# Two token parts from the input projection on, and 224 gathered tokens, in a hybrid decoder step with attention, recurrence and 16384 experts

## The chip, the cores and the metric

The kernel runs on one core of a Trainium2 chip. The metric is the device time of one execution in microseconds (us). The core's engines are TensorE (PE in the profile, its weight loads PEld), VectorE (DVE), ScalarE (ACT), GpSimd (POOL) and SyncE (SP), whose queue issues most DMAs.

## The reference, cut to what matters

One decoder layer is applied to 512 prompt tokens and 32 sample tokens (8 sequences of 4), 544 in all, with a model width of 2048.

```python
h = rmsnorm(x)                          # all 544 tokens
q, k, v, iq, ik, iw, xb, yb, qm = split(h @ w_in)
# A) each query scores all earlier keys (16 small heads), keeps the best 128 and attends to them;
#    sample tokens see 512 cached keys as well
# B) width-4 causal convolution of xb, two gates, linear recurrence over time, times gelu(yb)
# C) attention of qm to 256 memory tokens, 4 heads
m = sum(sigmoid(h @ w_gate[n]) * (branch[n] @ w_br[n]) for n in range(3))
x = x + m @ w_o
z = rmsnorm(x); q = z @ w_peer_q        # 8 heads x 2 halves x 128
# per head and half: top 16 of 128 keys; top 16 of the 256 sums -> 16 experts of 16384 per head
act = gelu(peer_u[e] . z);  x = x + sum(softmax(score) * act * peer_v[e])
y = rmsnorm(x)
```

The outputs are y, and keys, values, indexer keys, convolution and recurrence states and the memory's keys and values.

## The kernel before

All matrices are kept with tokens as columns. A float32 product is made of three TensorE products: `split` (L218) makes a high half on ScalarE (`hi`, L219) and a low half on VectorE (`lo`, L220), and high x high, high x low and low x high are summed in PSUM. `stream` (L236) loads 128 x 1024 weights (512 KB) through SP's queue and splits them. `project` (L254) takes two such loads for 2048 inputs; each of its 16 blocks gives three matmuls per group of token columns. 544 tokens are two halves of 272 columns, `xF` and `xA` (L303 to L306).

The order of work is that of the program text. Work in generators is woven in by `Background` (L138): `pump` is called once for each of the 8 blocks of a weight load and adds an eighth of `rate` steps; three queues (`bg`, `bg2`, `bg3`) have rates of their own, and `drain` runs what is left of one. `urgent` (L222) puts instructions ahead of others that are ready.

The stages, in order:

- Memory keys and values, with the first norm behind them.
- Input projection: 45 blocks of 128 outputs (`in_proj`, L400), both halves of tokens for each weight. Memory attention (`mem_head`, `mem_sample`), the scores and choice of keys (`dots`, `select_prompt`, `select_sample`), attention (`attn_head`, `attn_sample`) and the recurrence (`lru`) are background work of all tokens. It is drained at L644 and at L819.
- First half: `merge` (L833) of the three branches with their gates, `output_proj` (L875), then the query projection and the expert choice, `Route` (L950), of 256 of the 272 tokens; the other 16 queries are kept (`qk`). `lists` finds the top 16 of 128 keys per head half and tile of 128 tokens, `head` combines two lists. `pairs` (L1064) projects the queries and lets at most three `head` generators wait.
- Second half: merge and output projection. In its first branch (`after_merge`, L1183) the first choice is drained and the gather begins.
- Gather (`gathered`, L1115): the first 192 tokens don't go through all experts. Their rows of u and v are fetched by indirect DMAs issued by GpSimd (L1094), 128 rows of 8 KB each, and VectorE multiplies and sums them (L1142, L1150). 128 tokens take 128 slots; 64 tokens lie twice on the partitions and take 64. It is background `bg3`: a step fetches one slot's rows and works on one fetched two steps ago. `pace` ties a step to the last matmul.
- Second choice: the other 288 tokens in three tiles, the queries interleaved with `up` (L1215), the product of an expert block of 128 with the remaining 352 tokens. 50 of 128 ups are stored to DRAM ahead.
- Gate matrices (`gate_matrix`, L1227): for each token a one-hot product (L1259) spreads 128 weights over 128 x 128 experts, four tokens to a PSUM bank, which ScalarE copies into `gs` with another order (L1260).
- Dense experts: 16 rounds of 8 ups, the gating (`gated`, L1326) and the down products (`down`, L1344, matmul L1353) of 352 columns; last the norm and the output.

## Time and profile before

| | us |
|---|---|
| median of 3 runs | 4478.11 |
| lowest and highest | 4473.07, 4478.17 |
| profiled execution, its time | 4504.29 |
| profiled execution, its span | 4502.5 |

The span is from the first to the last instruction of one execution. The profile gives the busy time of each engine, the chain of work that ended last (followed back from the last instruction), groups of instructions by line with the mean duration of one, and the busy times in chosen stretches together with the granted clock of TensorE and the busy share of the 16 DMA engines. Matmuls follow each other before the one ahead has left the array, so the pace of a matmul is taken from the length of a chain piece over its count, not from the duration of one.

### The profile page before, as it was taken

To read this page: it belongs to the slowest core of one execution; us is meant where nothing else is said; L and a number is where in the kernel's file an instruction comes from. 1 tells how busy PE (TensorE), PEld (TensorE's weight loads), DVE (VectorE), ACT (ScalarE), POOL (GpSimd) and SP (SyncE) were. 2 spreads that over 40 slices of the span, in tenths; PEclk is the share of its full clock that TensorE was granted. 3 is DMA by queue.
4 is the path that set the end of the run, shared out by engine and by line. 5 is a ranking of instruction groups with operands and counts; after the bars stand their busy time and mean duration, and the time that the engine had idled before them with its cause. 6 is when DMAs were issued, how large, how long until landed. Compare 5 with 4: busy or idle time off the path is not lost.

```text
span 4502.5 us, 74141 instructions
## 1 busy us (share of the span) xinstructions
PE 4299.6 (95%) x29249; PEld 4130.8 (92%) x29249; DVE 3214.8 (71%) x4876; ACT 1823.1 (40%) x2732; POOL 1228.6 (27%) x1072
## 2 busy tenths in 40 slices
PE   8999989999999989998899899899999999999998
PEld 7986878789999989998888899899999999999998
DVE  6334825344456887887788776788888887888886
ACT  6232226544344434444332896222333333333333
POOL 3001110410001333533243101233343332344333
PEclk9999999999999999999999999999999999999999
DMA  8423443355556559998755676999999988999994
GB/s 267 164 85 116 145 131 107 120 161 185 178 183 209 166 165 336 360 351 302 273 169 168 208 253 238 352 343 330 335 337 349 349 309 302 349 345 345 347 352 154
DMA packets 342447, 1118.56 MB, mean 248 GB/s; under 512 B 42641, under 2 KB 137745, under 8 KB 289361
## 3 DMA queue, kind: packets, MB, share of 16 engines
q1 hardware_dynamic: 282704, 700.65, 45.8%
q0 software_dynamic: 59392, 413.17, 24.9%
q8 instruction: 229, 3.75, 0.3%
q14 instruction: 122, 0.99, 0.1%
HBM read 1050.75 MB, written 62.87 MB: 247 GB/s over the span
## 4 chain that ended last, share of the span: by engine, by line
PE 81%; DVE 7%; DMA 4%; issue 3%; ACT 2%; POOL 2%; another core or an unknown queue 1%; SPq 0%; DVEq 0%; POOLq 0%; ACTq 0%
PE mm L269 54%; PE mm L1353 19%; DVE lo L220 2%; PE w L1259 1%; PE mm L370 1%; PE w L556 1%; DMA gl<-ge_dram 1%; DMA x2r<-x_dram 1%; POOL eq L1017 1%; PE w L499 1%; POOL cand L1003 1%; ACT hi L219 1%; DVE eq L1015 1%; PE w L797 0%
## 5 line engine op out<-in xcount | busy, mean ns | idle before, releaser
L219 ACT CAST hi<-raw 128x1024 fp32r<-128x1024 f32 x1050 | 1096.8, 1049 | 1722.5 <-PE mm L269 898.8
L220 DVE TENSOR_TENSOR lo<-raw,hi 128x1024 fp32r<-128x1024 f32 x1050 | 1310.8, 1251 | 593.5 <-ACT hi L219 565.2
L269 PE MATMUL mm<-xgd,hi 128*128 128x352 f32 (+1 forms) x4608 | 1109.3, 324 | 10.5 <-ACT hi L219 10.5
L269 PEld LDWEIGHTS mm<-xgd,hi 128*128 128x128 f32 x4608 | 799.5, 189 | 14.3 <-ACT hi L219 12.4
L269 PE MATMUL mm<-xgd,lo 128*128 128x352 f32 (+1 forms) x2304 | 744.3, 323 | 32.9 <-DVE lo L220 32.9
L269 PE MATMUL mm<-xF,hi 128*128 128x272 f32 x2976 | 701.5, 295 | 2.8 <-issue 2.1
L1353 PE MATMUL mm<-zh,hi 128*128 128x352 f32 x2048 | 664.0, 326 | 29.3 <-ACT zh L219 20.9
L269 PE MATMUL mm<-xA,hi 128*128 128x272 f32 x2976 | 688.4, 290 | 1.7 <-ACT hi L219 1.3
L1353 PE MATMUL mm<-zh,lo 128*128 128x352 f32 x2048 | 664.0, 325 | 3.7 <-DVE lo L220 3.7
L1353 PE MATMUL mm<-zl,hi 128*128 128x352 f32 x2048 | 665.2, 325 | 1.8 <-DVE zl L220 1.8
L1094 POOL DMA_INDIRECT row<-in_un,idx x192 | 377.8, 1968 | 851.4 <-PE mm L269 333.7
L1094 POOL DMA_INDIRECT row<-in_vn,idx x192 | 391.0, 2036 | 680.8 <-PE mm L269 238.3
L269 PEld LDWEIGHTS mm<-xF,hi 128*128 128x128 f32 x2976 | 514.4, 189 | 39.2 <-issue 36.4
L269 PEld LDWEIGHTS mm<-xA,hi 128*128 128x128 f32 x2976 | 516.0, 190 | 10.5 <-issue 7.5
L1142 DVE SCALAR_TENSOR_TENSOR row<-row,xnat 128x2048 f32<-128x2048 f32 x192 | 440.2, 2293 | 64.2 <-DMA row<-in_un,idx 19.6
L1150 DVE SCALAR_TENSOR_TENSOR gacc<-row,hv,gacc 128x2048 f32<-128x2048 f32 x190 | 446.5, 2350 | 37.1 <-PE mm L269 13.9
L269 PEld LDWEIGHTS mm<-xgd,lo 128*128 128x128 f32 x2304 | 434.4, 189 | 38.2 <-DVE lo L220 37.9
L269 PE MATMUL mm<-xA,lo 128*128 128x272 f32 x1488 | 434.2, 292 | 10.0 <-DVE lo L220 9.9
L269 PE MATMUL mm<-xF,lo 128*128 128x272 f32 x1488 | 432.3, 291 | 0.0
L1353 PEld LDWEIGHTS mm<-zh,hi 128*128 128x128 f32 x2048 | 387.4, 190 | 33.5 <-ACT zh L219 23.3
L1353 PEld LDWEIGHTS mm<-zh,lo 128*128 128x128 f32 x2048 | 387.9, 190 | 5.5 <-DVE lo L220 5.5
L1353 PEld LDWEIGHTS mm<-zl,hi 128*128 128x128 f32 x2048 | 387.9, 189 | 3.2 <-DVE zl L220 2.9
(365 smaller groups left out, 6215.6 us busy)
## 6 DMA issues: line engine op xcount, KB each, us to landing
raw<-in_u SPq DMA_DIRECT2D x256, 512.0 KB
raw<-in_v SPq DMA_DIRECT2D x256, 512.0 KB
raw<-in_w_gate SPq DMA_DIRECT2D x192, 512.0 KB
raw<-in_w_br SPq DMA_DIRECT2D x96, 512.0 KB
raw<-in_w_in SPq DMA_DIRECT2D x90, 512.0 KB
raw<-in_w_pq SPq DMA_DIRECT2D x64, 512.0 KB
raw<-in_w_o SPq DMA_DIRECT2D x64, 512.0 KB
g_dram<-gs SPq DMA_DIRECT2D x11, 2048.0 KB
```

The lines of the kernel that those rows point to most:

```text
L219: nc.scalar.copy(hi, src)
L220: eng.tensor_tensor(lo, src, hi.bitcast(F), op=OP.subtract)
L269: last["mm"] = nc.tensor.matmul(p[:, i, :n], a[:, s], chunk(b[which], u + k), start=(u + k == 0 and pr == 0), stop=(u + k == k_chunks - 1 ...
L370: nc.tensor.matmul(p[:, mt], a[:, k, m], w[:, i * 512:(i + 1) * 512], start=(k == 0 and pr == 0), stop=(k == ND - 1 and pr == 2))
L499: nc.tensor.matmul(p[32 * c:32 * c + 32, j * 256:(j + 1) * 256], eT[:, i, 32 * h:32 * h + 32], cv[:, i, h * 256:(h + 1) * 256], start=(i = ...
L556: nc.tensor.matmul(p[:, :nk], s[r, P0 + qb * 128:P0 + qb * 128 + 128], ik2[r, P0:P0 + nk], start=True, stop=True)
L1003: nc.gpsimd.tensor_tensor(c2[:, :, :, off:off + n], lists[1][:, :, :, :n], lists[0][:, :, :, i:i + 1].to_broadcast([128, 2, nt, n]), op=OP ...
L1015: nc.vector.tensor_tensor(eq, iota[:, None, :ncand].to_broadcast([128, 16, ncand]), F16[:, t, :, None].to_broadcast([128, 16, ncand]), op= ...
L1094: i = nc.gpsimd.indirect_dma_start(out=r, out_offset=None, in_=ins[table], in_offset=bass.IndirectOffsetOnAxis(ap=ind[:, s:s + 1], axis=0))
L1142: j = nc.vector.scalar_tensor_tensor(r, r, 1.0, xn, op0=OP.mult, op1=OP.mult, accum_out=h)
L1150: j = nc.vector.scalar_tensor_tensor(acc, r, h, acc, op0=OP.mult, op1=OP.add)
L1353: last["mm"] = nc.tensor.matmul(p[:, 0, :NTA], a[:, s], b, start=(k == 0 and pr == 0), stop=(k == 7 and pr == 2))
```

## The change

Tokens are cut into 288 (32 sample and 256 prompt tokens, `HA`) and 256 (`HB`) instead of 272 and 272. The whole input projection with its attention, memory and recurrence work becomes a function `branches(part)`, called for part 0, then merge, output and expert choice of the first part run, and then `branches(1)`. What the second part needs of the first (keys, values, indexer keys, the last convolution inputs, the recurrence state) is kept in SBUF. Each weight of the input projection is streamed once for each part. The first choice has three tiles (128, 128, 32 tokens) and the second two, and `qk` goes. The gather starts in `branches(1)`, at the fourth memory head. 224 tokens are gathered in units of 128, 64 and 32, the last with four copies of the tokens on the partitions; 320 go through the dense experts. In the gate matrices the four tokens of a bank are written interleaved. Rates of the background queues and some extra buffers change.

```diff
-HT = T // 2
+HA = NS + SEQ // 2
+HB = T - HA
-NG = 192
+UNITS = ((0, 128, 1), (128, 64, 2), (192, 32, 4))
+NG = 224
...
+    kps = ExitStack()
+    kp_ = pool("keep", kps, side="right")
+    kT = kp_.tile([128, 2, T], F, name="kT")
...
+    def branches(part):
+        first = part == 0
+        x, cols, p0, qbs = ((xF, slice(0, HA), P0, (0, 1)), (xA, slice(HA, T), 0, (2, 3)))[part]
+        pp = None if first else ps_p
...
         def in_proj(ch, dst):
-        p = project(ins["w_in"][ch], [xF, xA], ND)
+            p = project(ins["w_in"][ch], [x], ND, pp)
...
+        left = bg.queue[-1] if bg.queue else None
+        bg.rate = 1.1 if first else 2.0
+        for h in range(4):
+            if h == 3 and not first:
+                bg.drain(left)
+                route1.weights()
+                start_gather()
+                rps.close()
+                bg3.rate = 0.5
+                bg.rate = 1.0
...
-    bg2.rate = 3.3
+        bg2.rate = 1.8
...
+        bg.rate = 2.5
+        bg2.rate = 2.2 if first else 1.6
...
-    tiles1 = [(0, 128), (128, 128)]
-    tiles2 = [(0, 128), (128, 128), (256, 32)]
+    tiles1 = [(0, 128), (128, 128), (256, 32)]
+    tiles2 = [(0, 128), (128, 128)]
...
-    widen(wide, 1, 1)
-    pairs(route1, query1, lambda c: None)
+    widen(wide, 1, 0)
+    pairs(route1, lambda c: query(c, xgF), lambda c: None)
...
+    branches(1)
...
-    mA = merge(HT, xA, map_, "left", after_merge)
+    mA = merge(HA, xA, map_, "left")
...
             for j in range(4):
-                nc.tensor.matmul(p[:, j * 128:(j + 1) * 128], o2[:, j], o1[:, j], start=True, stop=True)
-            nc.scalar.copy(gs[:, :, q * 4:q * 4 + 4].rearrange("p i t -> p t i"),
-                           p.rearrange("p (t i) -> p t i", t=4))
+                nc.tensor.matmul(p.rearrange("p (i t) -> p i t", t=4)[:, :, j], o2[:, j], o1[:, j], start=True, stop=True)
+            nc.scalar.copy(gs[:, :, q * 4:q * 4 + 4], p.rearrange("p (i t) -> p i t", t=4))
...
-    bg.rate = 1.3
-    bg3.rate = 0.15
+    bg.rate = 1.2
+    bg3.rate = 0.3
...
-    bg3.rate = 0.3
+    bg3.rate = 0.7
     for j in ups:
         up(j)
...
     for g in range(16):
-        bg3.rate = 0.7 if 8 * g < AHEAD_UP else 0.74
+        bg3.rate = 0.68 if 8 * g < AHEAD_UP else 0.7
```

## Rows read from the trace of the kernel before

**Rows 1.** The page, its head and the engines' busy us, share, instructions.
```profile
span 4502.5 us, 74141 instructions
PE 4299.6 (95%) x29249; PEld 4130.8 (92%) x29249; DVE 3214.8 (71%) x4876; ACT 1823.1 (40%) x2732; POOL 1228.6 (27%) x1072
```
**Rows 2.** Chain that ended last: start us, us, what, count (256, 512, 272, 352, 352 columns).
```profile
38.36 31.55 PE mm L269 x263
72.23 42.34 PE mm L370 x186
955.29 526.61 PE mm L269 x4207
...
3742.66 16.94 DMA xnat<-xn_dram
4245.10 62.72 PE mm L269 x384
4307.82 61.47 PE mm L1353 x384
```
**Rows 3.** Stretches: engines' busy us (instructions), TensorE's granted clock, DMA share, GB/s.
```profile
114.00:955.00 841.00, 806.81 (x5424) 674.69 (x5423) 378.85 (x852) 309.94 (x502) 124.63 (x151) 0.98 0.39 124
1482.00:1612.00 130.00, 118.26 (x912) 115.98 (x911) 113.08 (x404) 51.25 (x100) 51.48 (x121) 0.97 0.48 147
1612.00:2060.00 448.00, 433.27 (x3415) 430.44 (x3414) 368.33 (x433) 193.91 (x250) 195.77 (x132) 1.00 0.87 318
2190.00:2500.00 310.00, 273.83 (x1794) 262.98 (x1795) 252.42 (x771) 96.45 (x147) 106.74 (x196) 0.97 0.50 164
2500.00:2758.00 258.00, 253.86 (x1773) 252.04 (x1772) 197.10 (x369) 251.21 (x527) 23.02 (x14) 0.99 0.69 243
2828.00:3200.00 372.00, 346.98 (x2070) 340.11 (x2071) 316.64 (x365) 111.17 (x138) 125.15 (x61) 0.97 0.95 342
3200.00:3650.00 450.00, 450.00 (x2783) 450.00 (x2782) 393.18 (x390) 148.28 (x179) 169.30 (x85) 1.00 0.94 346
```
**Rows 4.** Groups by line, VectorE, 3250 to 3650 us: busy us, mean ns, idle before.
```profile
L220 DVE TENSOR_TENSOR lo<-raw,hi 128x1024 fp32r<-128x1024 f32 x103 | 125.6, 1220 | 11.2 <-ACT hi L219 11.1
L1150 DVE SCALAR_TENSOR_TENSOR gacc<-row,hv,gacc 128x2048 f32<-128x2048 f32 x40 | 94.0, 2351 | 5.7 <-PE mm L1353 2.1 <-PE mm L269 2.0 <-DMA row<-in_vn,idx 1.4
L1142 DVE SCALAR_TENSOR_TENSOR row<-row,xnat 128x2048 f32<-128x2048 f32 x36 | 82.4, 2288 | 15.6 <-DMA row<-in_un,idx 7.6 <-PE mm L1353 5.6 <-PE mm L269 2.3
L1356 DVE TENSOR_TENSOR acc<-mm,acc 128x352 f32<-128x352 f32 x48 | 25.0, 520 | 10.1 <-PE mm L1353 10.1
```
**Rows 5.** Groups by line, VectorE, 1480 to 1660 us.
```profile
L1015 DVE TENSOR_TENSOR eq<-cst,f 128x800 f32<-128x800 f32 x16 | 20.2, 1280 | 0.1
L960 DVE FIND_INDEX8 j<-si,sc 128x8 uint32<-128x128 f32 x32 | 9.0, 282 | 0.0
L1019 DVE TENSOR_REDUCE ev<-eq 128x16 f32<-128x800 f32 x8 | 7.8, 971 | 3.3 <-POOL eq L1017 3.3
L960 DVE FIND_INDEX8 p<-t,cand 128x8 uint32<-128x50 f32 x16 | 3.2, 203 | 0.0
L960 DVE MATCH_VALUE_LOAD j<-si,sc 128x8 f32 x32 | 2.4, 74 | 0.0
```
**Rows 6.** Groups by line, ScalarE, TensorE and VectorE, 2500 to 2758 us.
```profile
L1260 ACT COPY gs<-w 128x512 f32<-128x512 f32 x87 | 94.7, 1096 | 0.9 <-PE w L1259 0.9
L219 ACT CAST hi<-raw 128x1024 fp32r<-128x1024 f32 x44 | 46.6, 1058 | 0.5 <-PE mm L269 0.5
L269 PE MATMUL mm<-xgd,hi 128*128 128x352 f32 x707 | 179.6, 336 | 0.0
L1259 PE MATMUL w<-o,o 128*128 128x128 f32 x700 | 94.3, 277 | 4.1 <-DVE o L1276 4.0
L1269 DVE TENSOR_TENSOR o<-cst,Ti 128x512 f32<-128x512 f32 x88 | 60.2, 684 | 3.0 <-PE w L1259 2.9
```
**Rows 7.** The stretch from 1950 to 2000 us, columns as in rows 3.
```profile
1950.00:2000.00 50.00, 50.00 (x400) 50.00 (x399) 46.15 (x48) 23.87 (x32) 22.00 (x15) 1.00 0.98 378
```

More of the change, by code (lines that the diff above doesn't have):

```diff
@@ L278, in inv_rms @@
             for i in range(2):
-                nc.tensor.matmul(acc[:, i, :HT], ones, ssum[:, i * HT:(i + 1) * HT], start=True, stop=True)
-            a, o = acc[:, :, :HT], halves(out)
+                nc.tensor.matmul(acc[:, i, :n // 2], ones, halves(ssum)[:, i], start=True, stop=True)
+            a, o = acc[:, :, :n // 2], halves(out)
         else:
@@ L392, in program @@
-    nc.sync.dma_start(c1, ins["cst"][:, CB:])
-    def k1(a, n, rows=slice(0, 128)):
-        return c1[rows, a - CB:a - CB + n]
-    def bt(a):
-        return a[:, :P0].rearrange("p (b t) -> p b t", b=NB)
-    def in_proj(ch, dst):
-        p = project(ins["w_in"][ch], [xF, xA], ND)
-        with urgent():
-            nc.scalar.copy(halves(dst), p)
-        nc.sync.dma_start(outs["proj"][ch], dst)
-    def staged(ch):
-        s = stg.tile([128, T], F, name="stage", bufs=5)
-        in_proj(ch, s)
-        return s
@@ L490, in mem_sample @@
             for i in range(2):
-                nc.tensor.transpose(p[:, i * 128:(i + 1) * 128], e[:, i * 128:(i + 1) * 128], ident)
-            eT = mp.tile([128, 2, SEQ], F, name="mpT")[:, :, :128]
-            nc.scalar.copy(eT, p[:, :MEM].rearrange("p (a b) -> p a b", a=2))
+                for k in range(5):
+                    r = slice(0, 128 if k < 4 else NS)
+                    nc.tensor.matmul(p[:64, i * 256:(i + 1) * 256], pT[r, k, 64 * i:64 * i + 64],
+                                     vp[i][:, k] if k < 4 else vS, start=(k == 0), stop=(k == 4))
@@ L494, in mem_sample @@
+            oN = bp.tile([64, 512], F, name="oN")
+            nc.scalar.copy(oN, p[:64])
             yield
-            p = ps_w.tile([128, 512], F, name="w1")
-            for h in range(4):
-                c, j = divmod(h, 2)
+            for n in range(2):
+                r = slice(32 * n, 32 * n + 32)
+                p = ps_w.tile([128, 512], F, name="w1")
                 for i in range(2):
-                    nc.tensor.matmul(p[32 * c:32 * c + 32, j * 256:(j + 1) * 256], eT[:, i, 32 * h:32 * h + 32],
-                                     cv[:, i, h * 256:(h + 1) * 256], start=(i == 0), stop=(i == 1))
-                if h == 1:
-                    yield
@@ L515, in mem_sample @@
-        nc.sync.dma_start(o_dram[16:24, :, :P0].rearrange("h p s -> p h s"), mT)
-    bg.rate = 1.0
-    for h in range(4):
-        qm = []
-        for i in range(2):
-            s = staged(CH_QM + 2 * h + i)
-            nc.vector.tensor_copy(qms[:, 2 * h + i], s[:, :P0])
-            qm.append(s)
-        bg.add(mem_head(h, qm))
-    bg.add(mem_sample())
-    ik = xp_.tile([128, T], F, name="ik")
-    in_proj(CH_IK, ik)
-    ik2 = xp_.tile([128, T], F, name="ik2")
-    nc.scalar.copy(ik2[0:64], ik[0:64])
@@ new lines, in branches @@
+        if first:
+            bg2.add(*[attn_sample(pr) for pr in range(NB // 2)])
+        bg.rate = 2.5
+        bg2.rate = 2.2 if first else 1.6
+        for c in range(8):
+            xb = staged(CH_XB + c)
+            yb = staged(CH_YB + c)
+            bg.add(lru(c, xb, yb))
+        bg2.drain()
+        bg.drain()
+        if first:
+            nc.sync.dma_start(o_dram[0:8, :, :P0].rearrange("h p s -> p h s"), osm)
+        else:
+            nc.sync.dma_start(outs["hout"].rearrange("c p n -> p c n"), hl)
@@ L831, in program, with merge @@
+        lrs.close()
+        br.close()
     GLAG = 2
-    def merge(c0, x, mp_, side, each=None):
+    def merge(c0, x, mp_, side):
         mo = ([], [])
+        n_ = x[0].shape[-1]
         os_ = ExitStack()
         op_ = pool(f"lm{c0}", os_, side=side)
-        m = [mp_.tile([128, HT], F, name=f"m{e}", tag="ml", bufs=ND + 1) for e in range(ND)]
+        m = [mp_.tile([128, n_], F, name=f"m{e}", tag="ml", bufs=ND + 1) for e in range(ND)]
         for i, n in enumerate((2, 0, 1)):
-            op = ([op_.tile([128, HT], R, name=f"oh{k}") for k in range(8)],
-                  [op_.tile([128, HT], R, name=f"ol{k}") for k in range(8)])
+            op = ([op_.tile([128, n_], R, name=f"oh{k}") for k in range(8)],
+                  [op_.tile([128, n_], R, name=f"ol{k}") for k in range(8)])
@@ L902, in program @@
     xgfp = pool("xgf", xgfs, side="right")
-    xgF = [xgfp.tile([128, ND, HT], R, name=f"xgF{i}") for i in range(2)]
-    output_proj(0, mF, xgF, 0, rs[:, :HT])
+    xgF = [xgfp.tile([128, ND, HA], R, name=f"xgF{i}") for i in range(2)]
+    output_proj(0, mF, xgF, 0, rs[:, :HA])
     mfs.close()
@@ L1123, in gathered @@
             xn = gp.tile([128, D], F, name="xnat")
[L1124 to L1125 removed]
+            for a in range(0, 128, n):
+                nc.sync.dma_start(xn[a:a + n], xn_dram[c0 - 128:c0 - 128 + n])
         nb = slots // blk
```

906 lines of the change are left out of this document (471 added, 435 removed).

## The prediction

> **What bounds the kernel now.** I read the page first. Its profiled execution spans 4502.5 us, of which TensorE is busy 95% [rows 1]; that run took 4504.3 us as a whole, and the median of the runs shown is 4478.1, so 26 us below it. My sum is made against 4502.5 us and its difference is then put on the median.
>
> Next comes the chain of work that ended last, for the pace of TensorE where nothing interrupts it [rows 2]. Dividing each piece by its count gives one matmul of 256 columns 120.0 ns, of 272 columns 125.2, of 352 columns 163.3 in the up products and 160.1 in the down products, of 512 columns 227.6. From 272 to 512 that is 0.427 ns a column, close to one column per cycle at 2.4 GHz (0.417), with about 12 ns on top. Weight loads are as many as matmuls and stay beneath them.
>
> Then the busy times by stage [rows 3]: input projection with the attention behind it (114 to 955 us), second merge (1612 to 2060), the expert choice of the two halves (1482 to 1612 and 2190 to 2500), gate matrices (2500 to 2758), the first part of the down products, reading stored ups (2828 to 3200), and the loop of ups and downs (3200 on). The reader is to see two things. In the long stages TensorE is full. But VectorE stands at 87% in both the first expert choice and the loop, and DMA at 0.94 to 0.95 of its share with 342 to 346 GB/s. So TensorE is the bound with two followers close behind, and the change takes work from TensorE and gives work to both.
>
> **The change, part by part.** (1) *Dense experts.* The gathered tokens go from 192 to 224, so the dense matmuls go from 352 to 320 columns. 128 ups and 128 downs of 48 matmuls each are 12288 matmuls; 32 columns at 0.417 ns are 13.3 ns, in all 164 us off the path. By the step from 272 to 352 columns [rows 2] a column is 0.476 ns (up) or 0.436 (down), so up to 179 us. I take 164: ups 149.9 ns, downs 146.7.
>
> The Trainium skill, "TensorE: Matmul & The Clock Gate", section on the back-to-back issue gap, speaks against this: in a stream of weight load and matmul pairs it gives about 81 ns at 128 columns and 131 at 512, so 0.13 ns a column, and 32 columns would save only about 51 us, by which my sum below would end at 4533 (an estimate from that page). The 120, 125, 163 and 228 ns of this trace disagree.
>
> (2) *The extra gathers.* Slots go from 128 + 64 to 128 + 64 + 32, each with a row of u and one of v: 64 more rows of 128 x 8 KB. On VectorE a row costs 2.32 us, the mean of the two kinds [rows 4], so 148 us; GpSimd pays about 2 us each for issuing, and has time (169 of 450 us [rows 3]). Each is 1.05 MB, in all 67 MB.
>
> (3) *The input projection in two parts.* 45 chunks x 48 x 2 matmuls stay 4320, now 288 and 256 columns. 288 columns cost 125.2 + 16 x 0.417 = 131.9 ns, so a pair costs 251.9 ns where it cost 250.4: 3 us here; the merge, output and query matmuls were split before and go from 272/272 to 288/256, in all 7 us more. Of that the first part gets 4224 x 6.7 = 28 us more ahead, the second 22 us less. The weights are streamed twice: 90 more loads on SP's queue (47 MB), 90 more halvings on ScalarE and 90 x 1.22 = 110 us on VectorE. Small operations (recurrence, attention) come twice at half width.
>
> (4) *Order.* The gathers can start behind the first expert choice, which now lies ahead of the second part's projection, so about 39 of the 472 steps of the gather run there (78 weight streams x 0.5), 88 in the second merge and output, and the rate in the loop falls from 0.70/0.74 to 0.68/0.70. Counting streams times rates to the end gives 476 steps for 472, so nothing much is left over behind the last product.
>
> (5) *First choice with three tiles, second with two.* A tile costs VectorE per query chunk two searches, two maxima and a replacement with three loads, 5 x 0.28 + 3 x 0.07 = 1.6 us; per head the same five over a list of 50 at 0.2 each with loads, 1.24, then 1.28 and 0.97, together 3.5 us [rows 5].
>
> (6) *One-hot products.* TensorE writes PSUM with a stride of four, ScalarE reads it straight and writes runs of four. The copy takes 1.10 us [rows 6] where the plain copy to the high half, of twice the size, takes 1.06 [rows 6], so it should come down to about 0.6, for 80 copies instead of 88: up to 45 us of ScalarE, which is busy 251 of 258 us there [rows 3]. No strided TensorE write is in the trace; I bound it by 0 and by a doubling of 640 matmul records at 0.115 us (74 us), a gain being excluded as the columns stay as many, and take 0, since a write stays one element per column. (The 0.115: TensorE's 253.9 us [rows 3] less 707 and half as many again of 352 columns at 163.3 ns, over 700 records [rows 6].) The copy's bounds are 0.5 and 1.1 us. One group of 32 tokens less spares 64 records, 7 us.
>
> **The sum by stage** (before to after, profiled us).
> - Input projection, 841. Before, 4320 x 125.2 = 541 us are streams and 300 attention on TensorE and its stalls. I split these by keys and sample tokens (an estimate): 87 of matmuls to the second part, 195 with stalls to the first, which becomes 285 + 195 = 480. Second part: TensorE 259 + 87 = 346. VectorE there: 110 for halvings; half of the 379 [rows 3] less as many halvings, about 140; three left-over heads at 11, 33; 39 rows, 92: 375, less some 6% by which successive instructions overlap (an estimate), 352. The engines come out level and the two places where a chain is drained stay, and I take 397. The start of the gather adds a wait: VectorE's copy of the reshuffled indices waits for small DMAs, and the low halves queue behind it; 0 to the 16.9 us of a reload that held the chain [rows 2], which I take as nothing, three weights being ready. Together 877: **+36** (bounds 0 to +80).
> - First merge and output: **+28**.
> - First choice, 130 us with VectorE at 113 [rows 3]. It gets 16 x 1.6 + 5 heads x 3.5 = 43 us more (three heads may stay behind), and nothing covers that: TensorE's own 101 us are shorter already. **+43** (20 to 65).
> - Second merge, 448: TensorE 3456 x 5.2 ns = 18 less, heads no longer in its way 13 less, DMA fuller 10 more: **-21**. Output: **-8** (768 x 5.2 ns = 4, and waits).
> - Second choice, 310 with VectorE at 252: a tile less (-50), twice the gathers (+25), so 227 against TensorE's 257 (768 x 120 ns, 22 ups at 7.2, some 8 of lists). TensorE loses 4 on queries and 21 ups x 48 x 13.3 = 13, and about 18 of its 36 us of idle: **-35** (-10 to -45).
> - Gate matrices, 258: VectorE 197 - 11 (8 of 88 one-hot pairs at 0.68 [rows 6] and as much again) + 15 more rows x 2.32 = 217 after the shorter halvings, TensorE 147 + 74 = 221. So VectorE takes ScalarE's place. At 92% it needs 236; later ups move in. **-12** (-30 to +10).
> - Dense part, 2828 to the end. TensorE gives 78 ups x 48 x 13.3 + 128 x 48 x 13.3 = 132. Taken back: for each of the first 50 expert blocks DMA needs 2 streams of 0.524 MB, 1.43 MB of gathers, 0.33 of gates and stored ups, 2.80 MB in 7.04 us, 398 GB/s, where 342 was reached with stalls [rows 3]. At 350 the 50 take 400 us instead of 352; before it lost some 32, so 16 more are lost. In the loop VectorE per block was 15.5 x 0.874 = 13.6 us, and loses 0.16 gathers x 2.32 and 0.17 for five tiles narrowed from 352 columns at 0.52 us [rows 4]: 13.0 in 14.2, 92%. DMA: 2.10 + 2.94 + 0.16 = 5.20 MB in 14.2 us, 366 GB/s. I take 14 us of stalls, and 10 for one more change of gather unit (its reload held the chain 16.9 us [rows 2]). **-92** (-132 to -20).
>
> All: 36 + 28 + 43 - 21 - 8 - 35 - 12 - 92 = -61, so 4478 - 61 = 4417, rounded to **4420 us**. What TensorE saves is thus mostly paid back on VectorE.
>
> **The rivals.** *A, all is covered.* VectorE and DMA run at 92% to 98% without holding TensorE. For it: from 1950 to 2000 us VectorE was at 92%, DMA at 0.98 and 378 GB/s, and TensorE never stopped [rows 7]. Against it: the first choice has no cover at all. Then only the matmuls count: -164 + 10 - 7, 4317, and with the first choice 4360.
>
> *B, VectorE becomes the bound everywhere: slower.* It can't hold more than the 87.4% of the loop, the highest share that TensorE stood over hundreds of us. Its place is every stage with gathers, and it decides as soon as VectorE's work exceeds 0.874 of TensorE's, which is so in five of them. First choice 175/0.874 = 200 (+27 on my sum), second part's projection +30, second choice +10, gates +13, the two dense parts 355/0.874 and 1019/0.874, +6 and +32: 118 more, 4538. Against it: [rows 7].
>
> *C, DMA saturates at the loop's 346 GB/s* [rows 3]. Second merge and output at 364 GB/s asked, 507 us: +26 against 10 counted; first 50 blocks 140 MB/346 = 405, +5; loop 406 MB/346 = 1172, against 1108 + 14: +50. Together about +71, 4490: about no change. Against it 378 GB/s in [rows 7]. The Trainium skill, "DMA: Bandwidth & Descriptors", section "Where 436 GB/s comes from", takes the HBM side, about 358 GB/s per core, to bind such transfers; by that the loop's stage would take 1134, near my own (an estimate from that page). The 378 of [rows 7] goes above it.
>
> *D, matmuls shorten less than their columns do*, weight loads setting part of the pace. The smallest step of the rows, from 256 to 272 columns, is 5.2 ns for 16 columns, 0.325 each; 12288 x 32 of these are 128, 36 less than counted: 4456. A pace set by the loads alone would save nothing and give 4584; the four durations of [rows 2], which grow all the way, exclude that. The page named under (1) lies between.
>
> **How the numbers follow.** My forecast 0.60 (alone 4370 to 4475), A 0.13, B 0.15, C 0.11, D 0.01. A measurement of this kernel tells 0.2%, 9 us, from no change. Faster: A, D, nine tenths of the forecast and a part of C, 0.71; same: 0.11; slower: B and parts of C, 0.18. The range runs from 4345, in the upper half of A, to 4510, past C and toward B; outside lie some 0.1 on either side.
>
> **What would show it.** Ups at 150 ns and downs at 147 in the chain; a first choice of about 173 us with VectorE near 90% and TensorE waiting for the low halves; a second part's projection near 397; gates without ScalarE at 97% and a copy near 0.6 us; the first 50 blocks with DMA at 0.95 or more and waits for stored ups. Wrong would be: TensorE full in the first choice, VectorE over 95% with no stalls, stalls throughout the loop, or products of more than 0.115 us each.

## The result and the profile after

| | before, us | changed, us |
|---|---|---|
| median of 4 runs each | 4476.32 | 4523.38 |
| lowest and highest | 4473.07, 4478.17 | 4521.56, 4533.72 |
| ratio, 95% interval | | 1.0111 (1.0093 to 1.0128) |
| span of the profiled execution | 4502.5 | 4520.5 |

The change makes the kernel 1.1% slower; 1.3% faster was forecast. The page's head, first the span, then busy us, share and instructions of each engine, answers [rows 1]:

```profile
span 4520.5 us, 75499 instructions
PE 4168.4 (92%) x29283; PEld 3998.3 (88%) x29283; DVE 3443.5 (76%) x5192; ACT 1930.1 (43%) x2940; POOL 1268.6 (28%) x1159
```

TensorE does have less to do, 131 us less. The time is longer all the same, so it idles more: 352 us of the span where it idled 203. Where it idles is told by the stretches that answer [rows 3]: the two parts' projections (602 us and 1838 us are their ends), the first choice between them (1167 to 1308), the second merge, the second choice, the gate matrices, and two stretches of the rounds. Columns are as in [rows 3].

```profile
118.00:602.00 484.00, 459.95 (x2997) 375.56 (x2995) 258.92 (x604) 234.56 (x389) 122.08 (x157) 0.98 0.61 195
1167.00:1308.00 141.00, 127.96 (x895) 121.24 (x893) 127.22 (x501) 52.83 (x112) 44.89 (x110) 0.94 0.48 146
1308.00:1838.00 530.00, 390.69 (x2577) 341.60 (x2576) 383.63 (x747) 241.89 (x359) 122.58 (x135) 0.85 0.58 200
1838.00:2246.00 408.00, 401.96 (x3376) 401.19 (x3377) 355.37 (x324) 181.31 (x230) 188.61 (x99) 0.99 0.95 361
2380.00:2667.00 287.00, 247.48 (x1782) 242.55 (x1780) 242.77 (x582) 95.40 (x134) 96.95 (x167) 0.96 0.66 223
2667.00:2879.00 212.00, 211.49 (x1573) 210.12 (x1574) 204.85 (x355) 198.20 (x479) 63.31 (x27) 0.99 0.90 337
2968.00:3340.00 372.00, 337.97 (x2159) 330.99 (x2160) 317.88 (x368) 113.51 (x142) 100.74 (x61) 0.94 0.94 346
3340.00:3790.00 450.00, 444.09 (x3017) 442.99 (x3016) 393.21 (x439) 165.41 (x213) 136.00 (x93) 0.99 0.92 344
```

The third line is the case. The second part's projection takes 530 us in which TensorE is busy 391, VectorE 384 (72%), and DMA 0.58 of its share. No engine is full, and TensorE's granted clock is 0.85. Compare the gate matrices (2667 to 2879): VectorE is busy there 205 of 212 us, 97%, and TensorE still 211.

The profile of before was taken where that kernel took 4504 us, the one above where it takes 4476. The levels differ between chips, and the changed kernel, run once more beside a before of 4502.5 us, took 4544.7 (its span 4542.8). That run is the last column, the one to compare with the profile of before:

| stage | before | forecast | changed | changed, beside 4502 |
|---|---|---|---|---|
| input projection, first part | 841 for both | 480 | 484 | 508 |
| input projection, second part | | 397 | 530 | 535 |
| first merge and output | 527 | +28 | 565 | 565 (+38) |
| first choice | 130 | +43 | 141 | 140 (+10) |
| second merge | 448 | -21 | 408 | 409 (-39) |
| output | 130 | -8 | 134 | 134 (+4) |
| second choice | 310 | -35 | 287 | 287 (-23) |
| gate matrices | 258 | -12 | 212 | 211 (-47) |
| ups up to the first down | 70 | 0 | 89 | 89 (+19) |
| dense part from the first down | 1674 | -92 | 1552 | 1550 (-124) |

At the like level that is +202 for the projection and -162 for the rest, in all the 40 us between the spans of 4502.5 and 4542.8.

### The profile page after: what moved, and what is told of

It is laid out like the page before. It is cut to its first block, busy times and chain, and to the rows that moved or that the text cites. A ratio compares the mean times of both kernels' runs of the same rounds, so it can differ in the third digit from the quotient of the medians.

```text
span 4520.5 us, 75499 instructions
## 1 busy us (share of the span) xinstructions
PE 4168.4 (92%) x29283; PEld 3998.3 (88%) x29283; DVE 3443.5 (76%) x5192; ACT 1930.1 (43%) x2940; POOL 1268.6 (28%) x1159
## 5 line engine op out<-in xcount | busy, mean ns | idle before, releaser
L222 DVE TENSOR_TENSOR lo<-raw,hi 128x1024 fp32r<-128x1024 f32 x1140 | 1424.0, 1253 | 440.2 <-ACT hi L221 430.2
L271 PE MATMUL mm<-xgd,hi 128*128 128x320 f32 (+1 forms) x4608 | 1011.7, 309 | 4.0 <-ACT hi L221 4.0
L271 PE MATMUL mm<-xgd,lo 128*128 128x320 f32 (+1 forms) x2304 | 711.6, 309 | 21.1 <-DVE lo L222 21.0
L1400 PE MATMUL mm<-zh,hi 128*128 128x320 f32 x2048 | 638.8, 313 | 44.4 <-ACT zh L221 40.2
L1400 PE MATMUL mm<-zh,lo 128*128 128x320 f32 x2048 | 638.2, 313 | 9.8 <-DVE lo L222 9.6
L1400 PE MATMUL mm<-zl,hi 128*128 128x320 f32 x2048 | 638.1, 312 | 1.6 <-DVE zl L222 1.6
L271 PE MATMUL mm<-xF,hi 128*128 128x288 f32 x2976 | 624.2, 303 | 2.1 <-ACT stage L424 1.4
L271 PE MATMUL mm<-xA,hi 128*128 128x256 f32 x2976 | 550.7, 287 | 27.9 <-ACT hi L221 18.4
L271 PE MATMUL mm<-xF,lo 128*128 128x288 f32 x1488 | 445.7, 300 | 0.0
L271 PE MATMUL mm<-xA,lo 128*128 128x256 f32 x1488 | 426.7, 287 | 10.4 <-DVE lo L222 10.3
```

What stands on the lines that cost most here:

```text
L222: eng.tensor_tensor(lo, src, hi.bitcast(F), op=OP.subtract)
L271: last["mm"] = nc.tensor.matmul(p[:, i, :n], a[:, s], chunk(b[which], u + k), start=(u + k == 0 and pr == 0), stop=(u + k == k_chunks - 1 ...
L1400: last["mm"] = nc.tensor.matmul(p[:, 0, :NTA], a[:, s], b, start=(k == 0 and pr == 0), stop=(k == 7 and pr == 2))
```

## The experiments

The theory with which I went in: the second part's projection is held by serial chains of small operations, whose cost doesn't halve with the tokens (table loads of ScalarE, the merge's loads put ahead, left-over list combinations), and the gather's steps lie beside them. The rival: the gather's steps, 39 of them in this stage, take VectorE or DMA from the projection. From the first product on the second part's tokens to the end of its drained chains, the stage is 530 to 535 us; the expectations count to the first branch product of the merge behind it, 545 to 551. Each run is a single execution where no ratio is given.

**The gather taken out of the second part.**

```diff
                 start_gather()
                 rps.close()
-                bg3.rate = 0.5
                 bg.rate = 1.0
```

> The changed kernel with the gather's rate at 0 inside the second part's projection: some 39 steps, each a fetch of 1.05 MB and one VectorE pass of 2.3 us, leave that stage and are made up at the end of the kernel, so the total is longer by up to 110 us and only the length of the second part's projection counts (530 us in the changed kernel, 397 forecast). Theory 1 (serial chains with a fixed cost for each operation hold the stage, the gather is beside them): it stays at 500 to 530. Theory 2 (the gather's rows take VectorE and DMA from the projection): it falls to 400 to 450.

The stage as a stretch:

```profile
1332.00:1764.00 432.00, 365.48 (x2576) 325.84 (x2574) 305.46 (x684) 239.32 (x356) 65.56 (x96) 0.93 0.50 152
```

432 us, 103 less than the 535 of the changed kernel beside it; to the first branch product 447. The total, 4544.1, has 104 us of gather made up behind the last product, and says nothing. My theory falls: the gather's steps are not beside the chains, they cost 2.6 us each, more than VectorE's pass lasts. The 2576 matmuls are the same, but TensorE is busy 365 us instead of 396 for them, the mean granted clock being 0.93 instead of 0.85: up to 31 of the 103 us are matmuls that run longer. How much of that was on the path was not measured.

**The changed kernel again, and the two halves of a gather step.** The first is the changed kernel as it is. The second keeps the fetches and cuts VectorE's passes, the third keeps the passes and leaves out the fetches.

> The changed kernel itself once more, beside the three that follow on the same chip, since the runs without the gather and without the table loads had a first part some 24 us longer than the changed kernel's profile shows. If that is the chip, it shows here too: first part (first product to the first branch product of its merge) 520 to 530 instead of 502, second part (first product on its tokens to the first branch product of its merge) 535 to 555.

```diff
...
+                if only["part"] and (table == "un" or s):
+                    r, xn_, acc_ = r[:, :64], xn[:, :64], acc[:, :64]
                 if table == "un":
-                    j = nc.vector.scalar_tensor_tensor(r, r, 1.0, xn, ...)
+                    j = nc.vector.scalar_tensor_tensor(r, r, 1.0, xn_, ...)
...
```

> The changed kernel; the rows that the gather fetches inside the second part's projection are fetched in full, but VectorE's pass over each is cut from 2048 to 64 columns, so those rows are left out of the sums. The second part took 545 us with the gather and 446 without (first product on its tokens to the first branch product of its merge). Theory V (VectorE's passes of 2.3 us sit in its queue ahead of the low halves and of the chains' small steps): 450 to 480. Theory D (the 1.05 MB fetches hold back the weights): 515 to 550.

```diff
...
-                rows.append(rows_of(order[i][0], ind, order[i][1]))
+                if only["part"] and len(only["rows"]) == 3:
+                    rows.append(only["rows"][i % 3])
+                else:
+                    rows.append(rows_of(order[i][0], ind, order[i][1]))
...
```

> The changed kernel; inside the second part's projection VectorE makes all its passes of 2048 columns, but over the same three rows, so that all fetches but three are left out there (and those experts' values with them). Theory V (VectorE's passes): the second part stays at 515 to 550. Theory D (the fetches hold back the weights): 450 to 480. If both this run and the one without passes lie near 490 to 500, each has about half.

The stage in the changed kernel again:

```profile
1328.00:1864.00 536.00, 396.02 (x2575) 346.28 (x2574) 383.95 (x747) 241.28 (x359) 123.51 (x135) 0.84 0.58 198
```

with the fetches alone:

```profile
1329.00:1790.00 461.00, 376.50 (x2577) 334.10 (x2576) 314.19 (x746) 242.46 (x361) 106.25 (x135) 0.91 0.68 231
```

and with the passes alone:

```profile
1320.00:1832.00 512.00, 388.55 (x2582) 341.99 (x2580) 383.22 (x751) 242.47 (x359) 65.80 (x99) 0.85 0.43 136
```

Without the passes 75 us less, without the fetches 24 less, without both 103. So three quarters are VectorE's passes. VectorE's busy time falls by 70 us from the first row to the second, and the stage by 75: they are on the path in full, though VectorE is busy only 72% of the stage. To the first branch product the three kernels take 551, 476 and 526, so the passes fit theory V. The expected 515 to 550 for the passes alone and 450 to 480 for the fetches alone both came in. The first part took 526 us here to its first branch product, 24 more than in the first profile of the same kernel; with passes alone it took 518, though nothing differs there, so the first part varies by some 10 us from run to run.

The waits of TensorE and ScalarE tell how (changed kernel, 1308 to 1838 us; total us, times, longest):

```profile
PE w L483 <- DVE mex L455: 37.4, 3, 20.1
PE w L802 <- DVE ex L455: 33.6, 10, 4.9
PE w L792 <- DMA qh<-out_proj: 14.5, 1, 14.5
...
PE mm L271 <- DVE lo L222: 9.5, 10, 2.4
...
ACT hi L221 <- DMA raw<-in_w_in: 71.9, 33, 5.8
ACT oh L221 <- DMA oraw<-o_dram: 20.7, 5, 12.7
```

without the gather:

```profile
PE w L483 <- DVE mex L455: 21.0, 4, 18.5
...
PE w L791 <- DMA qh<-out_proj: 2.3, 1, 2.3
...
PE w L801 <- DVE ex L455: 1.5, 4, 0.7
...
ACT hi L221 <- DMA raw<-in_w_in: 38.1, 16, 4.5
```

and for `ex` with the fetches alone, then with the passes alone:

```profile
PE w L802 <- DVE ex L455: 5.6, 7, 2.8
```
```profile
PE w L802 <- DVE ex L455: 37.1, 10, 5.2
```

An attention head is a chain: product, maximum on VectorE, exponential on ScalarE, a reciprocal and a scaling on VectorE (`ex`, L455), transposes on TensorE. Each VectorE step of 0.15 to 0.6 us can now come behind a pass of 2.3 us, and the transposes with it stand in TensorE's order ahead of projection products, which themselves wait for low halves only 9.5 us in all. TensorE waits 33.6 us for `ex` where it waited 1.5, and 37.1 with the passes alone, 5.6 with the fetches alone. The memory heads (`mex`) are such a chain too, 37.4 us for 21.0; with `qh`, 14.5 for 2.3, these three waits make 60 of the 73 us that TensorE idles more. One wait for `mex` of 20.1 us is not the gather's: without the gather it is still 18.5, and the left-over list combinations below account for them. Behind the chains the fetches show: ScalarE waits 72 us for the weights of the projection instead of 38. VectorE's groups of the stretch (busy us, mean ns, idle before) show the passes, 37 of full cost, next to the 94 low halves:

```profile
L222 DVE TENSOR_TENSOR lo<-raw,hi 128x1024 fp32r<-128x1024 f32 x94 | 120.3, 1281 | 32.8 <-ACT hi L221 32.4
L1190 DVE SCALAR_TENSOR_TENSOR row<-row,xnat 128x2048 f32<-128x2048 f32 x24 | 54.8, 2282 | 1.9 <-DMA row<-in_un,idx 1.3 <-PE mm L271 0.5
L1198 DVE SCALAR_TENSOR_TENSOR gacc<-row,hv,gacc 128x2048 f32<-128x2048 f32 x13 | 30.5, 2344 | 2.1 <-PE mm L271 2.1
```

**The recurrence without table loads**, with the gather and without it.

```diff
-                nc.scalar.activation(g, p[:, :n_], AF.Sigmoid, bias=v(bcol))
+                nc.scalar.activation(g, p[:, :n_], AF.Relu, bias=v(bcol))
...
-            nc.scalar.activation(ig, yb, AF.Gelu_apprx_tanh)
+            nc.scalar.activation(ig, yb, AF.Relu)
```

> The changed kernel with sigmoid, tanh, exponential, square root and gelu of the recurrence all replaced by Relu: same instructions, same widths, but ScalarE needn't reload its function tables between them; the recurrence's values are left out by that. Theory 1 (part of the loss is table loads of 1.28 us that come once for each part whatever the width): ScalarE's table loads fall from 119 to under 40, the second part's last section (XB and YB chunks, 158 us) falls by 30 to 60 us, the first part's by as much, total 4420 to 4470. Theory 2 (VectorE and DMA hold that section): within 15 us of the changed kernel, 4508 to 4530.

ScalarE's table loads fell from 119 to 30, 89 x 1.283 = 114 us of ScalarE, and the total only from 4544.7 to 4529.0 (before: 4505.3); the second part, to the first branch product, from 551 to 527, and the first not at all (529 for 526). The first expectation failed. The second, within 15 us of the changed kernel, was missed by under a us in the total, less than single runs differ by, so the total decides nothing. The stage says more: 24 us, and at one place. 400 us into it TensorE has made as many products in both kernels (2199 and 2206); what differs is its end, where chains are drained (the changed kernel, columns as before):

```profile
1780.00:1800.00 20.00, 10.09 (x24) 5.57 (x22) 8.10 (x28) 12.98 (x21) 1.80 (x4) 0.67 0.08 26
1800.00:1820.00 20.00, 8.19 (x20) 5.47 (x20) 6.15 (x18) 14.53 (x19) 1.87 (x5) 0.50 0.06 20
1820.00:1840.00 20.00, 2.05 (x4) 1.18 (x4) 5.89 (x16) 12.18 (x15) 1.46 (x4) 0.50 0.26 58
```

TensorE has a few small products left, falls to its lower level (0.5 of full speed, 1.2 GHz), and ScalarE is the busiest. DMA is hardly used either: the gather is advanced by weight loads alone, and in a drain there are none.

> The changed kernel without the gather's steps in the second part's projection (447 us there instead of 545 to 551), and with the recurrence's functions replaced by Relu, which leaves the recurrence's values out but keeps every instruction. In the run without the gather ScalarE was busy 17 to 18 of 20 us over the last 140 us of that stage, and TensorE stood nearly still in its last 40. If ScalarE's table loads hold that end: second part 400 to 425 us, near the forecast 397. If the drained chains themselves hold it, each step waiting for the one ahead: 435 to 450.

The stage, and 20 us at its end without the gather, first with the table loads, then without them:

```profile
1295.00:1707.00 412.00, 364.93 (x2579) 326.10 (x2577) 305.23 (x689) 180.15 (x311) 72.25 (x96) 0.96 0.51 157
```
```profile
1740.00:1760.00 20.00, 2.05 (x4) 1.18 (x4) 7.21 (x21) 16.83 (x21) 1.82 (x4) 0.50 0.08 21
```
```profile
1690.00:1710.00 20.00, 10.36 (x85) 10.05 (x83) 9.01 (x15) 9.06 (x14) 2.90 (x3) 0.85 0.78 232
```

412 instead of 432, to the first branch product 427 instead of 447: 20 us, between what the two theories gave. A part of the drain stays. This run stands beside a before of 4470.5 us, the 432 beside one of 4505.3. The changed kernel's own stage is 530 beside 4476 and 535 beside 4502, so some 5 of the 20 us may be the level.

**The left-over list combinations.** The last three `head` generators of the first choice run on in the second part, on VectorE. First they were only put ahead in the program text, then left out.

```diff
...
     bg2.drain()
+    bg.drain()
     wide.close()
...
```

> The changed kernel with the waiting list combinations of the first expert choice drained at its end, not inside the second part's projection. My sum gave the first choice 43 us more and it took 11 more, with three combinations left over. If their 11 us each are VectorE's and uncovered in either place: the first choice (first query product to the end of the drain) 25 to 40 us longer, the second part 20 to 40 us shorter than 551, the total within 15 us of the changed kernel's 4545 (before: 4502). If the second part covers them: the second part shorter by less than 15 us and the total 15 to 35 us longer.

The total was 4560.0 (before: 4503), the second part 540 us. Neither expectation held, since the edit did not do what it says: drained in the text, the combinations have no TensorE work, so TensorE went on with the projection as before, and on VectorE the low halves, being urgent, again went between them. The run decides nothing on their cost. It is the changed kernel once more in all but name, and 15 us longer in total, 5 in the stage, which is how far single runs of one kernel differ.

Left out, in the kernel without the gather's steps in this stage:

```diff
...
+            if self.t0 == 0 and h >= 5:
+                yield
+                nc.vector.tensor_copy(ev4[:, ts, h], ev4[:, ts, 0])
+                nc.vector.tensor_copy(gw4[:, ts, h], gw4[:, ts, 0])
+                return
...
```

> The changed kernel without the gather's steps in the second part's projection (447 us there), and with the last three list combinations of the first expert choice replaced by copies of the first one's result (the choice of three heads is left out). If these three, left over from the first choice, hold VectorE at the stage's start and with it TensorE (20 us idle there): second part 415 to 430 us. If something else holds that place (weights, the first memory heads): 440 to 450.

```profile
1307.00:1720.00 413.00, 368.73 (x2576) 325.28 (x2574) 277.51 (x590) 238.90 (x356) 30.91 (x39) 0.95 0.52 159
```
```profile
PE w L483 <- DVE mex L455: 3.1, 2, 2.7
```

413 instead of 432, to the first branch product 428: 19 us, and VectorE is relieved of 28. The level is that of the run above, so by itself the 19 could be some 5 less; but TensorE's waits for `mex` fall from 21.0 to 3.1 us, the one of 18.5 us being gone, and that is nearly all of it. The three combinations cost the second part 18 to 19 us.

**The merge's loads not put ahead.**

```diff
-            with urgent():
+            with ExitStack() if c0 and i == 0 else urgent():
                 for k in range(8):
                     raw = op_.tile(..., name="oraw", tag="sg", bufs=4)
```

> The changed kernel; the loads and high halves of the second merge's first branch are no longer put ahead of other ready instructions, so that they fall behind the second part's projection instead of into it, where ScalarE stood 20.7 us in five waits for them. If these waits are on the path: the second part 10 to 25 us shorter (520 to 535 of 545). If another wait ends last beside them (weights, the drained expert choice): within 8 us of the changed kernel.

The stage took 532 us beside the 535 of the changed kernel, so by its number the second expectation holds. But ScalarE still waited 25.1 us in 7 waits for these loads within it, so the edit didn't take the wait away, and what it costs stays open.

**The one-hot products alone**, in the kernel before.

> The kernel before with one part of the change alone: the four tokens of a bank written interleaved, ScalarE's copy reading them straight. My sum's step: the copy falls from 1.10 us to about 0.6 us, TensorE's records stay at their 0.11 us, ScalarE leaves 97% in the gate stage, and the stage (258 us, TensorE busy 254) gains the few us that TensorE had left: total 5 to 15 us below before. Rival, the strided write costs TensorE time: up to 0.115 us on each of 704 records, 20 to 80 us slower.

4496.4 against 4505.3, ratio 0.9984 (0.9970 to 0.9998). The copy, in the changed kernel and here, and TensorE's products of the changed kernel:

```profile
L1308 ACT COPY gs<-w 128x512 f32<-128x512 f32 x80 | 45.7, 573 | 5.4 <-PE w L1307 5.2
L1307 PE MATMUL w<-o,o 128*128 128x128 f32 x640 | 87.5, 276 | 0.0
```
```profile
L1260 ACT COPY gs<-w 128x512 f32<-128x512 f32 x88 | 51.1, 581 | 13.5 <-PE w L1259 13.2
```

0.58 us instead of 1.10 [rows 6], the products at 276 and 274 ns where they were 277: the strided write costs nothing that shows. From the first to the last one-hot product the stage takes 244 us instead of 251, as TensorE, which idled 4 us of it before, now never stops. The 9 us of the medians agree with that, but by their interval it is anything from 1 to 14.

**224 gathered alone**, in the kernel before: `UNITS` and `start_gather` as in the change, tokens, projection and the start of the gather as before.

```diff
-NG = 192
+UNITS = ((0, 128, 1), (128, 64, 2), (192, 32, 4))
+NG = 224
...
-    bg3.rate = 0.15
+    bg3.rate = 0.3
...
-    bg3.rate = 0.3
+    bg3.rate = 0.7
...
-        bg3.rate = 0.7 if 8 * g < AHEAD_UP else 0.74
+        bg3.rate = 0.8 if 8 * g < AHEAD_UP else 0.81
```

> The kernel before with 224 gathered and 320 dense columns alone: no parts in the input projection, the gather starts where it did (in the second merge), its rates raised to 0.3, 0.7, 0.8 and 0.81 so that 64 more rows fit behind it. Theory 1 (the dense step was sized right, the loss of the changed kernel lies in the second part's projection): ups and downs at 147 ns as in the changed kernel, 60 to 120 us faster than before, 4355 to 4415. Theory 2 (VectorE or the DMA queues are the bound as soon as 64 more rows fall into the stages behind the merge, so the early start of the gather was needed): stalls take back most of it, 4460 or more.

4451.4 against 4505.3, ratio 0.9878 (0.9851 to 0.9905): faster by 1.2%, on the 4505 level 54 us, somewhat less than the 60 to 120 of theory 1. From the first to the last down product it took 1603 us, 50 less than before's 1653, and the choice of experts (first product on the second part's queries to the first one-hot product) 382 instead of 337. So the early start of the gather wasn't needed. A stretch of its rounds:

```profile
3650.00:4050.00 400.00, 391.32 (x2622) 386.44 (x2621) 382.13 (x386) 134.86 (x167) 131.09 (x88) 0.99 0.99 389
```

VectorE 96% with the same passes, DMA 0.99 with 389 GB/s, and TensorE 98%. Here VectorE only halves weights and adds results ahead of need, and most of a pass of 2.3 us in between is absorbed (how much, the next run tells).

**The changed kernel with the gather later**: no step in the second part, rates of the run before.

```diff
-                bg3.rate = 0.5
                 bg.rate = 1.0
...
-        bg3.rate = 0.68 if 8 * g < AHEAD_UP else 0.7
+        bg3.rate = 0.8 if 8 * g < AHEAD_UP else 0.81
```

> The changed kernel with no gather steps inside the second part's projection, made up by the rates of the unsplit kernel with 224 gathered (0.8 and 0.81 in the rounds of down products for 0.68 and 0.70). The second part loses 100 us (551 to 447) as shown; the rounds took 1603 us in the unsplit kernel with these rates and 1530 in the changed one. If the passes are covered in the rounds in part only: 100 - 73, some 27 us below the changed kernel (about 4545 beside a before of 4502), so 0 to 0.7% slower than before. If the rounds take them without loss: 2% below the changed kernel, 1% faster than before. If they only move: 0.9% slower than before, as the changed kernel.

4484.8 against 4507.1, ratio 0.9960 (0.9942 to 0.9978). Three rates turn the slower kernel into a faster one, 60 us below the changed kernel's own second run (4544.7). The second part took 432 us, 103 less, and the rounds 1584 for 1530. A step that cost 2.6 us in the projection costs 54/39 = 1.4 us in the rounds, more than nothing. The gain lies between the first expectation and the second. From the first product to the first branch product the two parts take 518 and 447 us in this run, together 965, where before took 857. So the split costs 108 us in the projection with no gather step among them; the heads and the table loads explain some 35 to 40 of these.

**The gather's steps moved again**, in the unsplit kernel with 224 gathered and the one-hot products, and the same without moving them.

```diff
-    bg3.rate = 0.5
+    bg3.rate = 0.6
...
-    bg3.rate = 0.3
+    bg3.rate = 0.15
...
-        bg3.rate = 0.8 if 8 * g < AHEAD_UP else 0.81
+        bg3.rate = 0.72 if 8 * g < AHEAD_UP else 0.83
```

> The kernel before, unsplit, with two parts of the change: 224 gathered and 320 dense columns, and the interleaved one-hot products. Gather steps are moved out of the stage where VectorE's small steps hold TensorE (the second expert choice, rate back from 0.3 to 0.15) into the second merge (0.5 to 0.6), and 0.72 and 0.83 in the rounds of down products. If VectorE's passes cost time only where TensorE waits for chains of VectorE: the second choice takes 335 to 350 us instead of 382 (first product on the second part's queries to the first one-hot product), the merge stays at 435, and the total is 1.4 to 2.0% below before. If it is their number alone that counts: the time lost reappears in the merge and the rounds, and the total stays at 1.2% below before (1.0 to 1.3).

> The kernel before, unsplit, with 224 gathered, 320 dense columns and the interleaved one-hot products, rates of the gather as in the run with 224 gathered alone (0.5, 0.3, 0.7, 0.8, 0.81). That run was 1.22% faster than before, the one-hot products alone 0.16%. If the two add: 1.3 to 1.5% faster. In its gate stage (first to last one-hot product, 216 us) ScalarE was busy 99%; if VectorE, busy 88% there, ends last once the copy takes 0.58 us, nothing is added: 1.1 to 1.3%.

Moved: 4465.3, ratio 0.9904 (0.9880 to 0.9927). Not moved: 4413.9, ratio 0.9806 (0.9788 to 0.9823), the fastest of all, 1.9% below before. My expectation of the move was wrong: the choice fell from 382 to 354 us, but the merge (first branch product to first output product) rose from 435 to 456, the stages behind the choice from 247 to 277 and the rounds from 1596 to 1610. The other expectation is right in kind: the time reappears, and more of it than was won. Why was not run; I read it so that in the choice the ups fill TensorE's waits, and what the choice no longer takes in comes back behind it. And the two parts do more than add: 1.22% and 0.16% alone, 1.94% together. The gate stage shows why; with 224 gathered alone, with the one-hot products alone, and with both:

```profile
2554.00:2770.00 216.00, 204.00 (x1415) 186.51 (x1414) 190.76 (x339) 214.70 (x456) 32.87 (x24) 1.00 0.80 295
```
```profile
2515.00:2759.00 244.00, 244.00 (x1735) 243.94 (x1736) 191.67 (x359) 215.70 (x512) 35.34 (x13) 1.00 0.71 252
```
```profile
2549.00:2737.00 188.00, 188.00 (x1415) 185.44 (x1414) 186.98 (x339) 185.29 (x456) 34.57 (x23) 1.00 0.89 335
```

With fewer columns alone ScalarE is full (214.7 of 216), with the faster copy alone TensorE is (244 of 244); each part hits the other's bound. Together the stage takes 188 us, with three engines at 98% or more and no stall.

## Why the prediction was wrong

The step that failed is the second part's projection: "the engines come out level and the two places where a chain is drained stay, and I take 397". I had summed VectorE's work, 92 us of gather passes and 33 of left-over heads in it, to 352 us, set TensorE's 346 beside it, and let the two run next to each other. The work was sized within a tenth (VectorE was busy 384 us; 305 without the gather), its cover wasn't: the wait of one engine for the other inside the chains was put at nothing. In this stage TensorE works through chains that go over VectorE and back, and what is put into VectorE's queue delays their steps. The runs price it: 75 us for the passes, 24 for the fetches, 103 for both, 18 to 19 for the heads, 15 to 20 for table loads that come for each part at full cost. That leaves 393 to 399 of 535, and 397 was forecast; that the last two add was not run. Up to 31 of the 103 us are TensorE at a lower granted clock.

The forecast for the first part was wrong too, by 28 us (508 at the like level, 480 forecast). No run looked for the cause; the 484 of the first profile looks like a hit, but stands at a lower level than the rows that the forecast was made from.

Of the bounds, "0 to +80" for this term was too narrow by 122 us: 202 at the like level. It held only the reshuffle of indices as an unknown, and no row that prices a gather step in a stage of chains.

The other terms:
- Dense part: right in kind, larger. The chain of the changed kernel, start, us, what and count:

```profile
3293.89 12.24 DMA gl<-ge_dram
...
3599.54 56.32 PE mm L271 x384
3655.86 56.32 PE mm L1400 x384
```

56.32 us for 384 is 146.7 ns for ups and downs alike (149.9 and 146.7 forecast). Ahead of the rounds and in them -152 us came (the last three lines of the table) where -104 was forecast. I had given back 40 for DMA and stalls, counting with 350 GB/s; DMA can do more, as the page's row of GB/s shows (40 slices of 113 us; the last eight are rounds):

```profile
GB/s 259 216 200 218 162 158 173 166 172 192 174 147 204 271 241 147 254 368 366 364 318 247 225 231 352 371 344 352 341 304 308 371 371 372 368 373 263 380 374 181
```

Several of those slices have 368 to 380. The first rounds do stand at 0.94 of DMA's share and 346 GB/s, and in the chain a reload of stored ups (`gl`) holds TensorE there, as forecast. The Trainium skill's rate for closely following pairs ("TensorE: Matmul & The Clock Gate", section on the back-to-back issue gap) would have given 51 us for the columns (an estimate from that page). The pace in the chain disagrees: an up fell from 163.3 to 146.7 ns, a down from 160.1, together about 184 us for 12288.
- Gate matrices: -12 forecast, -47 measured. The copy came out as forecast (0.6, measured 0.57 us). But the stage holds 136 products of ups fewer than before (1573 - 640 for 1773 - 704), some 20 us, which come in the next stage and are the +19 there. So -28 is the gain, and the error VectorE "at 92%" as a ceiling: it stood at 97%, TensorE at 211 of 212 us.
- First choice: +43 forecast, +10 measured. VectorE was at 90%, as foreseen, but more of its work was put off than the three heads that the forecast had taken out. 39 list searches lie in this stage (28 before, 48 in all), and only 10 of the 24 comparisons with which 8 heads combine three tiles, as many as before; 14 come in the second part, nearly five heads. The two lines of this stage, and the second part's (1308 to 1440 us):

```profile
L1019 DVE FIND_INDEX8 j<-si,sc 128x8 uint32<-128x128 f32 (+1 forms) x39 | 10.9, 279 | 0.0
...
L1074 DVE TENSOR_TENSOR eq<-cst,f 128x800 f32<-128x800 f32 x10 | 9.7, 967 | 0.0
```
```profile
L1074 DVE TENSOR_TENSOR eq<-cst,f 128x800 f32<-128x800 f32 x15 | 16.0, 1081 | 0.0
```

  (One of the 15 begins in the first stage.) The last three heads cost the second part 18 to 19 us; what the others cost there was not run.
- First merge and output +28 against +38, second merge -21 against -39, output -8 against +4, second choice -35 against -23: together 16 us above the forecast.

The rivals: D is out by the chain's pace, C by 368 to 389 GB/s. A expected all to be covered; that is nearly so in the gate matrices, by half in the rounds (1.4 of 2.6 us a step stay), and not at all in the projection. B gave 4538, nearer than my own, by the wrong reason: its ceiling of 87.4% on VectorE and its price of 30 us for the second part are both refuted, VectorE holding 96% to 99% beside a TensorE at 98% to 100% in a stretch of the rounds and in the gates, while 72% were too much in the projection.

What is not told apart: the remaining drain at the end of the second part, the merge's loads ahead of it, the first part's 28 us, and what the nearly two left-over heads beside the last three cost.

## What to carry to other kernels

A busy share doesn't tell whether an engine has room: ask in each stage whether the bound engine's next instruction waits for small steps of the engine that gets more work. Where it does, background work is paid in full (2.6 us a step here), where the other engine only prepares ahead, about half of it (1.4). And take a change of several parts to pieces: the parts that lower two engines' work in the same stage were worth more together (1.9%) than alone (1.2% and 0.2%), and the third, the split, ate them all. About half of that is the early gather: with the gather later the split kernel is 0.4% faster than before, the unsplit one 1.9%.

## What the hardware showed

- With the same 2576 matmuls TensorE was busy 365, 376, 389 and 396 us as the stage grew from 432 to 461, 512 and 536 and TensorE idled more, its mean granted clock falling from 0.93 to 0.91, 0.85 and 0.84.
- ScalarE's table loads have one duration, 1283 ns, at 256 columns as at 544, and their number goes with the parts: 49 in the projection before, 48 in each part after, in all 76 and 119. The Trainium skill, "ScalarE: Activation LUTs", section "What ACT_TABLE_LOAD costs", has the same 1283 ns, with a drain of about as much behind it, by which 89 loads would be 237 us of ScalarE (an estimate from that page). The trace agrees on the 1283 and shows no such drain. Where nothing else is waited for, the function starts 0.01 to 0.02 us behind the load (start us, us), so that 89 loads are 114 us:

```profile
1771.55 1.28 ACT L757 ACT_TABLE_LOAD   x1
1772.85 0.42 ACT L757 ACTIVATE th<-th 128x256 f32<-128x256 f32 x1
1773.28 1.28 ACT L776 ACT_TABLE_LOAD   x1
1774.58 0.42 ACT L776 ACTIVATE g<-stage 128x256 f32<-128x256 f32 x1
```

  Taking them away shortened the stage that drains its chains by 15 to 24 us and the other part not at all, so most of them lay beside other work.
- Writing PSUM with a stride of four cost TensorE nothing that shows (276 ns for 277), and reading it straight halved ScalarE's copy (1096 to 573 ns).
- VectorE at 99.5% (187 of 188 us) beside TensorE and ScalarE at 100% and 98.6% did not make TensorE wait in the gate stage of the fastest kernel.
